# A hybrid encoder layer on one core: a pool for the ropes, z staging, u stores on ScalarE's queue and a pinned start

## The chip, the cores and the metric

The kernel runs on one core of a Trainium2 chip. A core has TensorE (PE, which multiplies matrices; its weight loads are listed apart as PEld), VectorE (DVE), ScalarE (ACT), GpSimd (POOL) and SyncE (SP), which work side by side and wait for one another by semaphores. DMA transfers are issued from the queues of SP, ACT and POOL. The metric is the device time of one execution in microseconds; given is the median of the runs. One further execution was profiled.

## The reference

One encoder layer is applied to two sequences, of 256 and 512 tokens (together 768 tokens, six tiles of 128), with the same parameters. The width is 1024, all in float32.

```python
h = rmsnorm(x); u, q, k, v, qm, gl = split(h @ w_in)
y = s5_forward(u) + s5_backward(u) + d * u          # 64 groups, 64 complex states each
z = gelu(y);  s5_out = z * sigmoid(z @ w_glu)
q, k = rope(rmsnorm(q)), rope(rmsnorm(k))           # 8 heads, each with two softmax maps
diff = rmsnorm((softmax(q1 k1) - lam * softmax(q2 k2)) @ v) * (1 - 0.2)
mem = softmax(rmsnorm(qm) @ rmsnorm(mem_k).T) @ mem_v     # 256 memory tokens for each sequence, 4 heads
merged = sum over the three branches of sigmoid(gl_n + b_n) * (branch_n @ w_branch_n)
x = x + merged @ w_out
x = x + (silu(g) * up) @ w_down,  where g, up = rmsnorm(x) @ w_gate_up
```

## The kernel before

Every dense product is made of three matmuls (`mm3`, L748): each factor is split into a high part (`hi`, rounded by ACT) and a low part (`lo`, the rest, by DVE), and hi*hi, hi*lo and lo*hi are summed in PSUM. Weights come through `WStream` (L504): `_dma` loads half a chunk (512 KB) on SP's queue, `_split` makes its two parts on ACT (L595) and DVE (L601), and `ahead` keeps loads and splits in front of their use.

The Python code is written in program order; the framework plans it. It follows a simulated time line and may let an instruction of an engine pass others that were written before it, where the data allow. The order so found is fixed in the program. `tc.keep_in_program_order` takes an instruction out of this freedom; `tc.issue_after` ties one behind another. A tile pool is a piece of on-chip memory with a fixed place: pools are stacked from the left and, with `side="right"`, from the right. A pool that is opened where a closed pool lay can be written only when the instructions that used the old one are done.

The stages, in order of time:

1. Start (L678 to L1016). Warm-up matmuls on the identity keep PE running (L678). The gain of the memory norm is transposed to a column (L982, L983). `mem_features` (L991) transposes the memory rows (`nT`), scales them with this column and splits them into `memThi` (ACT) and `memTlo` (DVE). `mem_k(0)` multiplies them with the first weights (`mk`).
2. Memory attention, with the projections of q and of u. `u_chunk` (L1070) computes u into a tile `ut` by groups (ACT or DVE copies out of PSUM), and `u_flush` (L280) stores the tile to a scratch in HBM. The first four tiles use a pool with two buffers, the last four a pool with one (`utp2`, L1097). PSUM kind "d", into which u goes, has three buffers.
3. The S5 scan, spread over the products of the gates (`gl`).
4. Differential attention. `qk_units` (L1180) projects q and k of a head, normalizes and rotates them into `rope` (L1195); `v_units` (L1212) projects v for two heads. `diff_attend` (L1257) is a generator that runs beside them, paced by `dat.tick`: `stack` transposes `rope` into `qst`, `kst` and `kl` (L1235), `scores` (`sc`, L1286), `transposes` (`aT`, L1309), `values` (`av`, L1323) and `finish` (`oT`, `do`, L1345 to L1347). `rope` lies in pool `dq1`; with `dq2` it belongs to `wctx`, which is closed after the last projection (L1422). The attention's other tiles belong to `dctx`.
5. The branches (L1494 on). `merged` (L1500, 24 KB in each of the 128 partitions) lies on the right, where `dq1` and `dq2` were. The memory branch (`branch(2, ...)`, L1584) runs together with the rest of the attention: its first chunk (L1526 to L1542) has four accumulators. Ahead of its last chunk `tail` (L1572) drains the attention, closes `dctx`, opens `x1` and `XB` and loads z from its scratch (`load_pair`, L1561, on POOL's queue) to split it. Rows 2, 3, 4 and 7 of z come through `zst`, three buffers of 3 KB for each partition, the others through `stg`. Then follow the gated product of z (`glu`), the other two branches, the output projection, and the feed-forward part.

Of the kernel before, what the change touches and what calls it, by code (L numbers as in the profile page):

```python
# [23 lines left out]
class S5:  # L24
# [255 lines left out]
    def u_flush(self, ut, mt):  # L280

        self.nc.sync.dma_start(self.u_scr[mt].rearrange("(j h) (g k) -> h g j k", j=8, k=NK), ut)
# [221 lines left out]
class WStream:  # L504
# [7 lines left out]
    def __init__(self, nc, tc, ctx):  # L512
        self.nc = nc
        self.praw = ctx.enter_context(tc.tile_pool(name="wraw", bufs=3))
        self.ph = ctx.enter_context(tc.tile_pool(name="whi", bufs=4))
        self.pl = ctx.enter_context(tc.tile_pool(name="wlo", bufs=4))
        self.sub = nc.vector
        self.by_dma = False
        self.half = None
        self.src = []  # L520
        self.raw = {}
        self.parts = {}
        self.n_dma = 0
        self.n_split = 0
        self.next = 0
# [57 lines left out]
    def _split(self):  # L583
        i, h = divmod(self.n_split, 2)
        self.n_split += 1
        kind = self.src[i][3]
        if kind == "w":
            return self._split_w(i, h)
        hi, lo = self.tiles(f"{i}_{h}")
        self.parts.setdefault(i, []).append((hi, lo))  # L590
        r = self.raw.pop(2 * i + h)
        if kind == "g":
            f = lambda t: t.rearrange("p (m h g) -> p m g h", h=16, g=8)
            hi, lo, r = f(hi), f(lo), r.rearrange("p (m g h) -> p m g h", g=8, h=16)
        self.nc.scalar.activation(hi, r, AF.Copy)  # L595
        if self.by_dma:

            self.nc.scalar.activation(lo, r, AF.Copy, scale=-1.0)  # L598
            self.nc.gpsimd.dma_start(lo, r.bitcast(F32R), accum_op=ALU.add)  # L599
            return  # L600
        self.sub.tensor_tensor(out=lo, in0=r, in1=hi.bitcast(F32), op=ALU.subtract)  # L601
# [25 lines left out]
def hybrid_block(ctx, tc, A, outs, consts):  # L627
# [51 lines left out]
    for _ in range(14):  # L679
        pe.matmul(warm[:, 0:128], env.ident, env.ident, start=True, stop=True)  # L680
# [295 lines left out]
    with tc.tile_pool(name="nrm", bufs=1) as pool, tc.tile_pool(name="nrmg", bufs=1) as pg:  # L976
# [5 lines left out]
        pe.transpose(ps[:, 0:8], grow, env.ident[0:8, 0:8])  # L982
        v.tensor_copy(gcol, ps[:, 0:8])  # L983
        xm = []
# [6 lines left out]
        def mem_features(t0, nt):  # L991
            nk = 4 // nt
            for k0 in range(0, 8, nk):
                ps = env.psb("nT")
                pv = ps.rearrange("p (k t) -> p k t", k=nk)
                for k in range(nk):
                    for t in range(nt):
                        c = 128 * (k0 + k)
                        pe.transpose(pv[:, k, 128 * t : 128 * t + 128], xm[t0 + t][:, c : c + 128], env.ident)
                for k in range(nk):  # L1000
                    sl = (slice(None), k0 + k, slice(128 * t0, 128 * t0 + 128 * nt))
                    split_evac(MT[0][sl], MT[1][sl], pv[:, k], gcol[:, k0 + k : k0 + k + 1])
                if t0 == 0:
                    W.ahead(0, 1 + k0 // 4)

        mem_features(0, 1)
        units = mem_k(0)
# [126 lines left out]
    k2 = dctx.enter_context(tc.tile_pool(name="da2", bufs=2))  # L1134
    q1 = wctx.enter_context(tc.tile_pool(name="dq1", bufs=1))
# [42 lines left out]
    RO, VV, ST, half = {}, {}, {}, {}  # L1178

    def qk_units(h):  # L1180
# [3 lines left out]
        for tt in range(TILES):  # L1184
# [7 lines left out]
            if tt == TILES - 1:  # L1192
                mean_eps(ss, TILES * 4, 64)
                rs = rsqrt(ss, TILES * 4, "qkrs")
                ro = q1.tile([128, TILES, 256], F32, name=uid("rope"), tag="rope")  # L1195
# [16 lines left out]
    def v_units(vp):  # L1212
        w = W.get()
        V = k2.tile([128, TILES, 256], F32, name=uid("V"), tag="V")
        VV[vp] = V
        for tt in range(TILES):
            ps = psd("v")
            dense_tm(ps, w, 0, 256, H, tt)
            act.activation(V[:, tt], ps[:, 0:256], AF.Copy)
            yield 1.0  # L1220
# [36 lines left out]
    def diff_attend():  # L1257
# [90 lines left out]

        for i in range(N + 5):
            h, tt = divmod(i, TILES)  # L1350
            while (i < N and h not in ST) or (2 <= i < N + 2 and (i - 2) // TILES // 2 not in VV):
# [142 lines left out]
    with ExitStack() as c5:  # L1494
# [64 lines left out]
        zst = zctx.enter_context(tc.tile_pool(name="zst", bufs=3, side="right"))  # L1559

        def load_pair(X, src, scale=None, more=()):  # L1561
# [10 lines left out]
        def tail(c):  # L1572
# [8 lines left out]
            load_pair(Z, z_scr, 0.5, (2, 3, 4, 7))  # L1581
# [367 lines left out]
```

## Time and profile before

| | us |
|---|---|
| median of 3 runs | 1748.81 (1747.99 to 1750.8) |
| the profiled execution | 1746.76 |
| its span, from the first to the last instruction | 1745.0 |
| busy in the span: PE, PEld | 1730.8, 1605.3 |
| busy in the span: DVE, ACT, POOL | 1262.2, 888.9, 269.7 |

In rows of a profile, L595 is a line of the kernel above; `wh<-wr` names the tile that is written and those that are read, without their numbers; x124 counts instructions. An engine's idle time is put down to what released it, as in `<-ACT wh L595`. A matmul's end is modelled, so one matmul looks longer than what it adds when others follow it closely. A DMA's row on a queue is its issue; its landing is told apart. The granted clock of TensorE was 1.000 over the execution.

### The profile page before, as it was taken

What the parts mean: (1) busy time and instruction counts of PE and PEld (TensorE: products, weight loads), DVE (VectorE), ACT (ScalarE), POOL (GpSimd) and SP (SyncE); (2) the same over time, 40 slices, a digit from 0 to 9 for tenths busy, and PEclk for the clock granted to TensorE, in tenths of its full rate; (3) what the DMA queues carried; (4) which work ended last, traced back from release to release, by engine and by line L of the source; (5) the groups of instructions that cost most, each with busy time, mean ns of one, the idle gap of its engine ahead of it and who ended that gap; (6) DMA issues with size and microseconds to landing.
All of it is one profiled execution on the core that took longest, in us unless ns stands there. A gap on an engine that the chain in (4) does not pass through costs nothing.

```text
span 1745.0 us, 29497 instructions
## 1 busy us (share of the span) xinstructions
PE 1730.8 (99%) x11236; PEld 1605.3 (92%) x11236; DVE 1262.2 (72%) x2353; ACT 888.9 (51%) x1868; POOL 269.7 (15%) x288
## 2 busy tenths in 40 slices
PE   9999999999999999999999999999999999999999
PEld 9999988999999999999989888888889999998887
DVE  7665649699999778887886445453598777776775
ACT  7444543776767346877765434232343333334443
POOL 0000000000000100111000002000036555541130
PEclk9999999999999999999999999999999999999999
DMA  7223636755566454645653437331312323238973
GB/s 270 75 85 97 127 114 132 182 125 147 143 159 159 115 143 101 161 97 153 165 164 109 133 115 249 116 117 62 87 65 91 109 91 109 91 110 283 259 159 95
DMA packets 209214, 234.11 MB, mean 134 GB/s; under 512 B 57832, under 2 KB 173296, under 8 KB 209072
## 3 DMA queue, kind: packets, MB, share of 16 engines
q1 hardware_dynamic: 190480, 170.73, 32.6%
q0 software_dynamic: 17440, 58.34, 15.4%
q10 hardware_dynamic: 1152, 3.15, 0.5%
q8 instruction: 89, 1.46, 0.4%
q14 instruction: 53, 0.43, 0.1%
HBM read 165.78 MB, written 41.22 MB: 119 GB/s over the span
## 4 chain that ended last, share of the span: by engine, by line
PE 95%; DVE 2%; DMA 1%; ACT 1%; issue 0%; SPq 0%; ACTq 0%
PE gl L751 4%; PE br L751 4%; PE br L752 4%; PE gl L753 4%; PE gl L752 4%; PE br L753 4%; PE gate L751 3%; PE up L751 3%; PE gate L753 3%; PE gate L752 3%; PE up L752 3%; PE up L753 3%; PE dn L752 3%; PE dn L753 3%; PE dn L751 3%; PE qk L752 3%
## 5 line engine op out<-in xcount | busy, mean ns | idle before, releaser
L595 ACT ACTIVATE wh<-wr 128x1024 fp32r<-128x1024 f32 x124 | 140.4, 1133 | 65.0 <-PE br L752 26.2
L601 DVE TENSOR_TENSOR wl<-wr,wh 128x1024 fp32r<-128x1024 f32 x82 | 108.5, 1324 | 81.8 <-ACT wh L595 80.0
L751 PE MATMUL gl<-H,wh 128*128 128x256 f32 (+1 forms) x384 | 132.0, 344 | 0.0
L753 PE MATMUL gl<-H,wl 128*128 128x256 f32 (+1 forms) x384 | 129.0, 336 | 0.0
L752 PE MATMUL gl<-H,wh 128*128 128x256 f32 (+1 forms) x384 | 128.7, 335 | 0.0
L599 POOL DMA_DIRECT2D wl<-wr x42 | 36.6, 872 | 504.7 <-ACT wl L598 486.9
L751 PE MATMUL qk<-wh,H 128*128 128x256 f32 x384 | 108.0, 281 | 0.0
L752 PE MATMUL qk<-wl,H 128*128 128x256 f32 x384 | 107.8, 281 | 0.0
L753 PE MATMUL qk<-wh,H 128*128 128x256 f32 x384 | 107.1, 279 | 0.0
L752 PE MATMUL dn<-wld,dxh 128*128 128x512 f32 x231 | 89.6, 389 | 0.0
L751 PE MATMUL dn<-whd,dxh 128*128 128x512 f32 x231 | 89.5, 389 | 0.0
L753 PE MATMUL dn<-whd,dxl 128*128 128x512 f32 x231 | 88.9, 389 | 0.0
L753 PEld LDWEIGHTS gl<-H,wl 128*128 128x128 f32 x384 | 72.0, 188 | 8.0
L752 PEld LDWEIGHTS gl<-H,wh 128*128 128x128 f32 x384 | 72.2, 188 | 7.2
L751 PEld LDWEIGHTS gl<-H,wh 128*128 128x128 f32 x384 | 72.3, 188 | 6.9
L557 ACT ACTIVATE wh_S<-ws 128x512 fp32r<-128x512 f32 x70 | 41.1, 625 | 65.2 <-PE up L752 36.8
L753 PEld LDWEIGHTS qk<-wh,H 128*128 128x128 f32 x384 | 72.3, 188 | 0.7
L751 PEld LDWEIGHTS qk<-wh,H 128*128 128x128 f32 x384 | 72.4, 188 | 0.6
L752 PEld LDWEIGHTS qk<-wl,H 128*128 128x128 f32 x384 | 72.2, 188 | 0.5
L1292 DVE TENSOR_REDUCE nm<-sc 128x1 f32<-128x512 f32 (+1 forms) x96 | 56.7, 597 | 18.4 <-PE sc L1287 17.6
L558 DVE TENSOR_TENSOR wl_S<-ws,wh_S 128x512 fp32r<-128x512 f32 x70 | 57.9, 850 | 15.9 <-ACT wh_S L557 15.9
L1294 ACT ACTIVATE p<-sc,nm 128x512 f32<-128x512 f32 (+1 forms) x96 | 58.8, 615 | 13.5 <-DVE nm L1292 13.0
(477 smaller groups left out, 6001.3 us busy)
## 6 DMA issues: line engine op xcount, KB each, us to landing
wr<-in_w_in_dram SPq DMA_DIRECT2D x48, 512.0 KB, 4.6
wr<-in_w_gate_up_dram SPq DMA_DIRECT2D x44, 512.0 KB, 3.6
wl<-wr POOLq DMA_DIRECT2D x42, 512.0 KB, 5.4
wr<-in_w_branch_dram SPq DMA_DIRECT2D x24, 512.0 KB, 4.7
glr<-gl_scr POOLq DMA_DIRECT2D x24, 384.0 KB, 3.9
hid_scr<-fa SPq DMA_DIRECT2D x11, 768.0 KB, 6.5
wr<-in_w_mem_kv_dram SPq DMA_DIRECT2D x16, 512.0 KB, 4.2
wr<-in_w_in_dram SPq DMA_DIRECT2D x32, 256.0 KB, 3.7
```

The lines of the kernel that those rows point to most:

```text
L557: self.nc.scalar.activation(f(hi), src, AF.Copy)
L558: self.nc.vector.tensor_tensor(out=f(lo), in0=src, in1=f(hi).bitcast(F32), op=ALU.subtract)
L595: self.nc.scalar.activation(hi, r, AF.Copy)
L599: self.nc.gpsimd.dma_start(lo, r.bitcast(F32R), accum_op=ALU.add)
L601: self.sub.tensor_tensor(out=lo, in0=r, in1=hi.bitcast(F32), op=ALU.subtract)
L751: pe.matmul(ps, wh, xh, start=start, stop=False, **kw)
L752: pe.matmul(ps, wh, xl, start=False, stop=False, **kw)
L753: pe.matmul(ps, wl, xh, start=False, stop=stop, **kw)
L1292: v.tensor_reduce(out=nm[:, m : m + 1], in_=ps, axis=AX.X, op=ALU.max, negate=True)
L1294: act.activation(pm[:, 0:n], ps, AF.Exp, bias=nm[:, m : m + 1], accum_out=s1s[:, tt : tt + 1] if m == 0 else s2)
```

## The change

Four things are changed, with what they need.

- `u_flush` issues its store from ScalarE instead of SyncE.
- The ropes get a pool of their own, `drope`, opened after `da2` and ahead of `dq1`, and closed with `dctx`.
- `zst` is no longer opened ahead of the memory branch but in `tail`, after `x1` and `XB`. Beside it, `diff_attend` asks for the tiles of V that a step reads (`values_there`), where it asked whether V was begun.
- At the beginning, nine of the 14 warm-up matmuls stay in their place and five follow the transpose of the gain; all of them and this transpose keep their order. For the first tile of the memory rows, the split of half a weight chunk is written ahead of the scaling of the four rows, and ACT's part of both keeps its order.

```diff
@@ u_flush
-        self.nc.sync.dma_start(self.u_scr[mt].rearrange("(j h) (g k) -> h g j k", j=8, k=NK), ut)
+        self.nc.scalar.dma_start(self.u_scr[mt].rearrange("(j h) (g k) -> h g j k", j=8, k=NK), ut)
@@ WStream
+        self.mark = lambda i: None
...
-        self.nc.scalar.activation(hi, r, AF.Copy)
+        self.mark(self.nc.scalar.activation(hi, r, AF.Copy))
@@ hybrid_block
     warm = env.psa("warm")
-    for _ in range(14):
-        pe.matmul(warm[:, 0:128], env.ident, env.ident, start=True, stop=True)
+
+    def warming(n):
+        for _ in range(n):
+            tc.keep_in_program_order(pe.matmul(warm[:, 0:128], env.ident, env.ident, start=True, stop=True))
+
+    warming(9)
...
-        pe.transpose(ps[:, 0:8], grow, env.ident[0:8, 0:8])
+        tc.keep_in_program_order(pe.transpose(ps[:, 0:8], grow, env.ident[0:8, 0:8]))
         v.tensor_copy(gcol, ps[:, 0:8])
+        warming(5)
@@ mem_features
+                if t0 == 0:
+                    W.ahead(0, 1 + k0 // 4)
                 for k in range(nk):
                     sl = (slice(None), k0 + k, slice(128 * t0, 128 * t0 + 128 * nt))
-                    split_evac(MT[0][sl], MT[1][sl], pv[:, k], gcol[:, k0 + k : k0 + k + 1])
-                if t0 == 0:
-                    W.ahead(0, 1 + k0 // 4)
-
+                    gk_ = gcol[:, k0 + k : k0 + k + 1]
+                    hi = act.activation(MT[0][sl], pv[:, k], AF.Copy, scale=gk_)
+                    if t0 == 0:
+                        tc.keep_in_program_order(hi)
+                    v.scalar_tensor_tensor(out=MT[1][sl], in0=pv[:, k], scalar=gk_, in1=MT[0][sl].bitcast(F32),
+                                           op0=mul, op1=sub)
+
+        W.mark = tc.keep_in_program_order
         mem_features(0, 1)
+        W.mark = lambda i: None
@@ pools of the attention
     k2 = dctx.enter_context(tc.tile_pool(name="da2", bufs=2))
+    rop = dctx.enter_context(tc.tile_pool(name="drope", bufs=1))
     q1 = wctx.enter_context(tc.tile_pool(name="dq1", bufs=1))
@@ qk_units
-                ro = q1.tile([128, TILES, 256], F32, name=uid("rope"), tag="rope")
+                ro = rop.tile([128, TILES, 256], F32, name=uid("rope"), tag="rope")
@@ v_units
         VV[vp] = V
+        V_TILES[vp] = 0
         for tt in range(TILES):
...
             act.activation(V[:, tt], ps[:, 0:256], AF.Copy)
+            V_TILES[vp] = tt + 1
             yield 1.0
@@ diff_attend
+        def values_there(i):
+            if not 0 <= i < N:
+                return True
+            h, tt = divmod(i, TILES)
+            return V_TILES.get(h // 2, 0) >= (2 if tt < 2 else TILES)
+
         for i in range(N + 5):
             h, tt = divmod(i, TILES)
-            while (i < N and h not in ST) or (2 <= i < N + 2 and (i - 2) // TILES // 2 not in VV):
+            while (i < N and h not in ST) or not values_there(i - 2):
                 yield
@@ the branches
         zctx = c5.enter_context(ExitStack())
-        zst = zctx.enter_context(tc.tile_pool(name="zst", bufs=3, side="right"))
-
-        def load_pair(X, src, scale=None, more=()):
+        def load_pair(X, src, scale=None, zst=None, more=()):
...
             Z = L["Z"] = pair(L["XB"], "z")
-            load_pair(Z, z_scr, 0.5, (2, 3, 4, 7))
+            zst = zctx.enter_context(tc.tile_pool(name="zst", bufs=3, side="right"))
+            load_pair(Z, z_scr, 0.5, zst, (2, 3, 4, 7))
             zctx.close()
```

More of the change, by code (lines that the diff above doesn't have):

```diff
@@ L1177, in hybrid_block @@
         gp.memset(t[64 - 64 * (i % 2) : 128 - 64 * (i % 2)].bitcast(F32), 0.0)
-    RO, VV, ST, half = {}, {}, {}, {}
+    RO, VV, ST, half, V_TILES = {}, {}, {}, {}, {}
     def qk_units(h):
```

## The prediction

> **What bounds the kernel now.** I read the page first, then busy time in stretches of 25 us, then the waits of PE (TensorE).
>
> ```profile
> span 1745.0 us, 29497 instructions
> PE 1730.8 (99%) x11236; PEld 1605.3 (92%) x11236; DVE 1262.2 (72%) x2353; ACT 888.9 (51%) x1868; POOL 269.7 (15%) x288
> ```
>
> PE is busy for 1730.8 of 1745.0 us. No edit changes what PE computes, so the change can win little more than the 14.2 us in which PE stands still, plus what PE loses while busy but badly overlapped. In the next rows the first number after the comma of a window is its length, then comes the busy time of PE, PEld (weight loads), DVE, ACT and POOL.
>
> ```profile
> 0.00:25.00 25.00, 21.67 (x159) 20.96 (x160) 13.96 (x33) 15.87 (x37) 0.71 (x6) 1.00 0.83 286
> 275.00:300.00 25.00, 22.94 (x137) 20.09 (x137) 24.60 (x54) 8.67 (x13) 1.61 (x11) 1.00 0.50 114
> 875.00:900.00 25.00, 24.01 (x191) 22.93 (x189) 22.70 (x53) 16.85 (x47) 1.11 (x2) 1.00 0.60 186
> 900.00:925.00 25.00, 22.95 (x160) 20.03 (x161) 21.75 (x57) 19.20 (x56) 3.86 (x7) 1.00 0.45 130
> 1725.00:1750.00 25.00, 15.86 (x70) 12.78 (x69) 5.95 (x8) 1.89 (x3) 0.00 (x0) 0.93 0.09 32
> ```
>
> The idle time stands in four places: 3.3 us at the start, 2.1 us in 275 to 300, 0.99 + 2.05 = 3.0 us in 875 to 925, and 25 - 15.86 - 5 (the span ends at 1745) = 4.1 us at the end, which no edit touches. These four are 12.5 of the 14.2 us.
>
> ```profile
> PE u L751 <- ACT ut L1080: 2.1, 1, 2.1
> PE nT L999 <- DMA nx<-in_mem_prompt_dram: 1.5, 1, 1.5
> PE warm L680 <- POOL ident masks.py:199: 1.4, 1, 1.4
> PE mk L753 <- DVE memTlo L746: 0.4, 1, 0.4
> ```
>
> **Ropes in a pool of their own.** In before, the rotated q and k of a head (`rope`, L1195) lie in `dq1`, and `merged` (L1500) is laid over `dq1` and `dq2` once these are closed. So the first merge (L1520) may not write before PE has transposed the last head's `rope` (L1235).
>
> ```profile
> L1235 PE MATMUL qkT<-ident,rope x96: 270/272/303, 650.3 to 910.0; 128*128 128x128 f32 x96
> L1520 DVE SCALAR_TENSOR_TENSOR merged<-glr,br x16: 376/552/689, 911.3 to 987.4; 128x256 f32<-128x256 f32 x8, 128x512 f32<-128x512 f32 x8
> L1208 DVE TENSOR_TENSOR rope<-rope,ropet x16: 648/950/1246, 638.6 to 889.6; 128x512 f32<-128x512 f32 x8, 128x1024 f32<-128x1024 f32 x8
> 880.00:896.00 16.00, 16.00 (x130) 15.57 (x130) 15.55 (x32) 8.73 (x24) 1.11 (x2) 1.00 0.72 222
> 896.00:912.00 16.00, 12.96 (x84) 10.06 (x83) 11.90 (x37) 14.27 (x46) 1.42 (x3) 1.00 0.08 28
> 912.00:928.00 16.00, 16.00 (x116) 14.94 (x115) 14.14 (x34) 9.43 (x22) 2.44 (x5) 1.00 0.72 214
> L1323 PE MATMUL av<-V,aT 128*128 128x128 f32 x32 | 4.7, 286 | 1.6 <-ACT aT L1311 1.6
> L1286 PE MATMUL sc<-kst,qst 128*128 128x512 f32 (+1 forms) x10 | 4.2, 424 | 0.6 <-ACT p L1294 0.6
> L752 PE MATMUL br<-H,wh 128*128 128x256 f32 x1 | 0.4, 365 | 0.0
> ```
>
> ```profile
> 890.17 0.12 PE br L752
> ```
>
> The rows fit: last transpose at 910.0, first merge at 911.3. The first chunk of the branch wants four PSUM accumulators (L1531 to L1535) and the kind "d" has three, so from 896 the branch stands still (one `br` matmul on L752 in 896 to 912) and PE runs attention alone, waiting for ScalarE. With the change, what `merged` covers is `dq1` without `rope` and `dq2`; their last use is L1208 at 889.6 + 1.2 = 890.8. The merges can then go from about 891, and three of the chunk's six products of 256 columns are still to be done: 3 x 24 matmuls at 0.12 us (what one adds to the chain of waits when others stand before and behind it, the row above; 365 ns is only its modelled length) is 8.6 us of filler, more than the gaps.
>
> What is won lies between 16.00 - 12.96 = 3.0 us (PE's plain idle time in 896 to 912) and 16.00 - 10.06 - 0.43 = 5.5 us (idle time of the weight loads, less the 0.43 us that they miss in 880 to 896). It can also be zero, if the branch only runs ahead and attention then ends as late as now. I take **4.0 us**, nearer the plain idle time. Lost against it are two merges of 0.4 us that DVE must now fit in earlier; DVE has 11.90 of 16 us there. The Trainium skill (Perfetto Trace Analysis, § Identifying the Most-Contended Engine) says that busy matmul time flatters PE and that weight-load time is the better measure; by it alone this term would be 5.5 us and the time 1.5 us lower. The two measures do part here (12.96 against 10.06 us busy); no run so far shows which of them a filled gap follows.
>
> **u stored by ScalarE's queue.** `u_flush` (L282) moves eight stores from SP's queue to ACT's. In the right-hand pool `utp2` there is one `ut`, so ACT may write the next only when the store has landed.
>
> ```profile
> 279.35 0.59 ACT L1080 ACTIVATE ut<-u 128x512 f32<-128x512 f32 x1
> 280.91 0.37 SPq L539 DMA_DIRECT2D wr<-in_w_in_dram  x1
> 281.39 8.10 DMA u_scr<-ut
> 289.58 0.88 ACT L1080 ACTIVATE ut<-u 128x256 f32<-128x256 f32 x2 [9.65 <-DMA u_scr<-ut]
> DMA to landing us min/median/max: 4.3/4.9/8.1
> L1347 ACTq DMA_DIRECT2D br_scr<-do x8: 326/326/344, 740.7 to 985.8; - x8
> ```
>
> `ut` is full at 279.94, but SP holds the store behind a weight load that itself waits for a buffer; it leaves at 281.39, lands 8.1 us later, and PE has waited 2.1 us. On ACT it can leave at 280.0, ahead of that load. Landing after 4.3 to 8.1 us gives 284.3 to 288.1; PE goes on when the first of the two copies at 289.58 ends, near 290.0, and has been ready since 290.0 - 2.1 = 287.9. With 0.4 us for a copy, the late landing leaves 0.6 us of the wait, the early one none: 1.5 to 2.1 us go. What ACT pays is 8 x 0.33 = 2.6 us of issue over some 80 us, in a stretch where it is busy for 8.67 of 25 us; queued behind an issue are weight splits and `ut` copies, each late by 0.33 us, for which PE waits next; with ACT idle for 16 of 25 us I let them be caught up. The bounds are 0 and 2.1 us. I take **2.0 us**. The rule against it: the Trainium skill (DMA: Bandwidth & Descriptors, § Issuing engines are not separate DMA queues) has transfers from all queues interleave on the same 16 engines, so that another queue saves issue time alone. By it the store still needs 8.1 us, this term is 1.5 us and the time 0.5 us higher; no row here separates the two.
>
> **Pinned order at the beginning.** Nine of 14 warm-up matmuls, then the transpose of the gain, then five; the first weight splits of ACT are planned before the four `memThi` of their half instead of anywhere, and their order is kept.
>
> ```profile
> 1.38 5.67 PE L680 MATMUL warm<-ident 128*128 128x128 f32 x28 [1.38 <-POOL ident masks.py:199]
> 7.03 1.06 ACT L595 ACTIVATE wh<-wr 128x1024 fp32r<-128x1024 f32 x1 [5.00 <-DMA wr<-in_w_mem_kv_dram]
> 8.45 1.06 ACT L595 ACTIVATE wh<-wr 128x1024 fp32r<-128x1024 f32 x1 [0.35 <-DMA wr<-in_w_mem_kv_dram]
> 9.52 0.63 ACT L745 ACTIVATE memThi<-nT,gmem 128x128 fp32r<-128x128 f32 x2
> ```
>
> ```profile
> 9.27 0.16 DVE L983 COPY gmem<-gT 128x8 f32<-128x8 f32 x1
> ```
>
> ```profile
> 8.20:11.10 2.90, 0.95 (x8) 0.72 (x7) 2.79 (x5) 2.10 (x5) 0.00 (x0) 1.00 1.00 400
> ```
>
> Nine of 14 take 5.67 x 9 / 14 = 3.6 us, so the gain's column is there at about 1.38 + 3.6 + 0.2 + 0.2 = 5.4 instead of 9.4, if its load has landed by 5.0; a later landing costs at most what the last five warm-ups are pushed past 7.1. ACT ends its first split at 8.1 and now does four `memThi` (0.31 us each) at once, where it waited for the second load until 8.45 and split it first: the first one at 8.1 instead of 9.52. But DVE is busy for 2.79 of 2.90 us in 8.2 to 11.1, and what it must do (two low parts, then the `memTlo`) is the same. So PE may fill its idle 1.5 + 0.4 us, or meet DVE's limit two microseconds later and win nothing. It could lose 1.2 us, four `memThi` ahead of the second split. I take **1.0 us** between.
>
> **z staging behind the attention.** `zst` is opened in `tail` after `x1` and `XB`, since three buffers of 768 x 4 bytes are 9 KB and the 6 KB of ropes now lie there.
>
> ```profile
> 910.55 1.71 POOL L1565 DMA_DIRECT2D brr<-z_scr  x3 [19.93 <-PE qkT L1235]
> 984.72 1.04 ACT L1346 ACTIVATE do<-oT,subg 128x256 f32<-128x256 f32 x2
> 986.38 3.04 ACT L745 ACTIVATE zhi<-brr 128x768 fp32r<-128x768 f32 x4
> ```
>
> ```profile
> L746 DVE SCALAR_TENSOR_TENSOR zlo<-brr,zhi x8: 948/950/959, 986.5 to 995.2; 128x768 fp32r<-128x768 f32 x8
> ```
>
> ```profile
> DMA to landing us min/median/max: 3.4/4.5/10.3
> ```
>
> ```profile
> 987.20:1004.00 16.80, 16.80 (x97) 14.70 (x97) 1.25 (x3) 1.00 0.70 222
> ```
>
> Three z loads go at 910.55 today, released by the same last rope transpose. At best the new place waits for the same thing; at worst for attention's end, the last `do` at 984.72 + 1.04 = 985.8. A load then lands at 985.8 + 4.5 = 990.3, ACT and DVE split it in 0.84 + 0.95, by 992.1; the gated product takes 16.8 / 8 = 2.1 us for a row of z, so from 987.2 it wants row 2 at 991.4. Cost 0.7 us at the median landing, 6.5 us at the longest (10.3). I take zero: the release is the same. The stricter test on V (`values_there`) asks for tiles that must have been written already for the result to be right; it delays nothing and I cost it at zero, at worst one unit of V (8 x 3 x 0.12 = 2.9 us) of other PE work earlier.
>
> **Sum.** 4.0 + 2.0 + 1.0 = 7.0 us. The profiled execution took 1746.76 us (1745.0 of span, 1.8 around it), 2.05 us under the median of 1748.81. So 1739.8 for such an execution and **1741.8 us** for the median.
>
> **Rivals.** (a) *The ropes win nothing*: the merges still wait for something else in that place, or ACT, busy for 14.27 of 16 us in 896 to 912, keeps attention's pace, and the branch that ran ahead is missing later. Then 3.0 us are left: 1745.8. For it: that ACT row. Against it: ACT has 9.43 of 16 us afterwards, so attention can catch up. (b) *Slower*: attention's end becomes the bound. The branch, used up at 896 to 912, no longer covers 976 to 987, and the four z loads issued only at 985.8 stand in that chain at their longest landing. 4.0 us of gain go, 6.5 us are added: 1746.76 - 3.0 + 6.5 + 2.05 = 1752.3, and 1754 if the eighth row, which waits for the third's buffer, costs 2 us more. It decides once the third z row lands after 991.4 - 1.8 = 989.6 and the branch has run dry before 985. Against it: today's loads wait for the rope alone. (c) *More*: 5.5 + 2.1 + 1.9 = 9.5 us: 1739.3, or less by what a newly planned order takes from attention elsewhere.
>
> **Chances.** Forecast 0.55 (own range 1739.8 to 1744.5), (a) 0.20, (b) 0.13, (c) 0.12. A measurement tells about 0.2%, 3.5 us, from no change: faster is below 1745.3, slower above 1752.3. Faster 0.55 + 0.12 + 0.03 of (a) = 0.70; same 0.17 of (a) and 0.03 of (b) = 0.20; slower 0.10. The range, 1738.0 (c less the 0.8 us by which the runs fall under their median, rounded) to 1748.5, holds the forecast, (a) and most of (c).
>
> **What would show it.** The first merge near 891 and `br` matmuls throughout 896 to 912, PE busy for nearly 16 of 16 us; no wait of `u` for `ut`; stores of u issued within 0.2 us of the copy; first `memThi` near 8.1; z loads near 905. A PE wait on `zlo` or `br` dry before 985 would make it wrong, as would new PE waits in places that no edit names.

## The result, and the profile after

The changed kernel takes 1753.22 us (median of 8 runs, 1751.87 to 1755.92), the kernel before 1748.45 us on the same chip (8 runs, 1747.99 to 1750.8). The ratio is 1.0029, 95% interval 1.0018 to 1.0040: some 5 us slower, where 7 us faster were forecast. Here and below a ratio compares a kernel with the kernel before in the same batch, is not quite the quotient of the two medians, and leaves out one slow execution of u alone (2438 us, granted clock 0.66).

The page of the changed kernel:

```profile
span 1753.7 us, 29486 instructions
PE 1736.8 (99%) x11236; PEld 1612.3 (92%) x11236; DVE 1265.0 (72%) x2353; ACT 890.0 (51%) x1868; POOL 269.0 (15%) x288
```

PE works on the same 11,236 matmuls, but counts as busy for 6.0 us more (1736.8 against 1730.8) and stands still for 16.9 us instead of 14.2. (The two profiled executions lie 8.75 us apart, 1755.51 against 1746.76, the medians only 4.8, so part of what this trace loses belongs to this one execution.) Where that is shows in its stretches of 25 us (columns as in the prediction; the number in front of the last two is the granted clock):

```profile
0.00:25.00 25.00, 20.35 (x115) 18.83 (x115) 10.87 (x26) 12.66 (x30) 0.71 (x6) 0.86 0.83 284
275.00:300.00 25.00, 25.00 (x147) 22.00 (x146) 23.34 (x77) 8.98 (x16) 0.55 (x9) 1.00 0.51 94
875.00:900.00 25.00, 25.00 (x202) 24.30 (x202) 21.25 (x51) 14.92 (x43) 1.11 (x2) 1.00 0.75 230
900.00:925.00 25.00, 25.00 (x188) 23.61 (x187) 17.47 (x47) 17.00 (x46) 1.65 (x3) 1.00 0.29 92
975.00:1000.00 25.00, 18.31 (x95) 15.81 (x94) 13.53 (x30) 11.96 (x25) 1.61 (x3) 0.80 0.35 121
```

The last of these stretches before the change:

```profile
975.00:1000.00 25.00, 25.00 (x143) 21.80 (x142) 15.72 (x29) 10.22 (x13) 2.69 (x5) 1.00 0.46 146
```

The two gaps that the change aimed at in the middle are closed: 22.94 became 25.00 in 275 to 300, and 875 to 925 is full. But the start has fewer matmuls (115 against 159) at a lower clock, and a new hole stands in 975 to 1000, which was full before. Three of the longest waits of PE name both places:

```profile
PE oT L1361 <- DVE osb L1353: 5.2, 1, 5.2
PE glu L756 <- ACT zhi L750: 1.5, 1, 1.5
PE mk L758 <- DVE memTlo L1014: 1.4, 1, 1.4
```

**The new hole, in order of time** (start, duration, engine, line, operation, idle time before it and what ended it):

```profile
983.97 0.39 PE L758 MATMUL br<-H,wl 128*128 128x512 f32 x1
...
984.21 1.05 PE L1339 MATMUL av<-V,aT 128*128 128x128 f32 x8
...
986.41 0.16 DVE L1348 TENSOR_TENSOR ssq<-ssq,r 128x6 f32<-128x6 f32 x1
...
989.42 0.96 DVE L1353 TENSOR_TENSOR osb<-osb,rqy 128x768 f32<-128x768 f32 x1
...
990.43 1.54 PE L1361 MATMUL oT<-ident,osb 128*128 128x128 f32 x6 [5.18 <-DVE osb L1353]
...
992.01 0.69 ACT L1362 ACTIVATE do<-oT,subg 128x512 f32<-128x512 f32 x1 [0.38 <-PE oT L1361]
992.60 0.83 ACT L750 ACTIVATE zhi<-brr 128x768 fp32r<-128x768 f32 x1
...
993.49 1.65 PE L756 MATMUL glu<-zhi,wh 128*128 128x256 f32 x4 [1.51 <-ACT zhi L750]
...
997.06 0.63 PE L758 MATMUL glu<-zhi,wl 128*128 128x512 f32 x1
```

The last `br` matmul goes at 983.97, the attention's last `av` right behind it. Then only the end of the attention is left, one thing after another: sum of squares, small steps of DVE from 986.41 to 989.42, the scaling of `osb`, its transposes, `do`, and only then the split of z, which lies where the attention's tiles were. PE has nothing to put into it. In before the last `br` (L753) went at 987.0, behind the last `oT`, so this chain was covered:

```profile
L1345 PE MATMUL oT<-ident,osb x10: 272/272/273, 960.4 to 984.1; 128*128 128x128 f32 x10
```

```profile
L753 PE MATMUL br<-H,wl x144: 276/280/480, 879.6 to 987.0; 128*128 128x256 f32 x96, 128*128 128x512 f32 x48
```

And the matmuls behind the hole of the changed kernel are slow: 0.63 us for one of 512 columns at 997.06, 0.39 us at 983.97.

### The profile page after: what moved, and what is told of

It reads as the page before. It is cut to its first block, busy times and chain, and to the rows that moved or that the text cites. A ratio compares the mean times of both kernels' runs of the same rounds, so it can differ in the third digit from the quotient of the medians.

```text
span 1753.7 us, 29486 instructions
## 1 busy us (share of the span) xinstructions
PE 1736.8 (99%) x11236; PEld 1612.3 (92%) x11236; DVE 1265.0 (72%) x2353; ACT 890.0 (51%) x1868; POOL 269.0 (15%) x288
## 4 chain that ended last, share of the span: by engine, by line
PE 96%; DVE 1%; DMA 1%; ACT 1%; issue 0%; SPq 0%; DVEq 0%; ACTq 0%
PE gl L756 4%; PE gl L757 4%; PE gl L758 4%; PE br L756 4%; PE br L757 4%; PE br L758 4%; PE gate L756 3%; PE gate L758 3%; PE up L756 3%; PE up L758 3%; PE gate L757 3%; PE up L757 3%; PE dn L758 3%; PE dn L757 3%; PE dn L756 3%; PE qk L758 3%
## 5 line engine op out<-in xcount | busy, mean ns | idle before, releaser
L1308 DVE TENSOR_REDUCE nm<-sc 128x1 f32<-128x512 f32 (+1 forms) x96 | 56.5, 597 | 17.8 <-PE sc L1303 16.9
```

The source lines that it names most:

```text
L1308: v.tensor_reduce(out=nm[:, m : m + 1], in_=ps, axis=AX.X, op=ALU.max, negate=True)
```

## The experiments

All kernels contain the edit to u's store, so what the other parts do is read against the first of them, u alone.

**1. The parts by themselves.** u's store alone:

```
-        self.nc.sync.dma_start(self.u_scr[mt]..., ut)
+        self.nc.scalar.dma_start(self.u_scr[mt]..., ut)
```

> The kernel before with the u store on ScalarE's queue alone. Theory: 2.1 us gained, 1748.45 - 2.1 = 1746.3, ratio 0.9988; the store that takes 8.1 us is issued within 0.3 us of its copy and PE does not wait for ut. Rival, that transfers interleave anyway and only the issue is earlier: 1.5 us, and PE still waits 0.6 us.

Measured: 1746.10 us, ratio 0.9989 (0.9979 to 0.9999). Run again in a later batch:

> u's store alone once more, beside the last one on the same chip: 0.9985 to 0.9993 of before.

Measured: 1745.34 us, ratio 0.9997 (0.9988 to 1.0006), above what was expected. Between them it wins 0.5 to 1.9 us; with two kernels below whose other edit shows no cost (0.9993 and 0.9992) the mean is 0.0007, 1.3 us. Its window, without a wait of PE for `ut`:

```profile
275.00:300.00 25.00, 25.00 (x145) 22.00 (x145) 24.60 (x54) 8.79 (x13) 2.48 (x11) 1.00 0.49 102
```

The store that took 8.1 us before, and the copy that waits for its landing:

```profile
280.13 0.37 ACTq L282 DMA_DIRECT2D u_scr<-ut  x1
286.84 0.88 ACT L1080 ACTIVATE ut<-u 128x256 f32<-128x256 f32 x2 [6.80 <-DMA u_scr<-ut]
```

It leaves within 0.1 us of its copy (279.45 + 0.60 = 280.05) and lands at most 6.7 us later. Five profiles with this store on ScalarE's queue (u alone twice, ropes and u, u with the pinned start, the changed kernel) have 5.7 to 6.7 us from its issue to the next copy. So it leaves sooner and also lands faster than the 8.1 us before; why it lands faster is not shown.

u's store with the ropes and z's staging, the start as before:

```
+    rop = dctx.enter_context(tc.tile_pool(name="drope", bufs=1))
-                ro = q1.tile(...)
+                ro = rop.tile(...)
-            while ... (i - 2) // TILES // 2 not in VV:
+            while ... not values_there(i - 2):
-        zst = zctx.enter_context(...)            # ahead of the branch
+            zst = zctx.enter_context(...)        # in tail, behind XB
```

> The change without its pinned start (u on ScalarE, ropes, z staging stay). Theory from the two traces: the pinned start costs 5.8 us (PE ends the first products at 157.6 instead of 151.8), so the time is 1753.2 - 5.8 = 1747.4, ratio 0.9994, and the first 25 us are as in the kernel before, granted clock 1.00. Rival, that the start is only shaken by a new plan and the pins as such cost nothing: 1753 again.

Measured: 1750.34 us, ratio 1.0017 (1.0008 to 1.0027). The ropes are not a gain: against u alone they cost 1.0017 - 0.9989 = 0.0028, 4.9 us (4.2 us by the medians of that batch). The rows of two tiles tell the same without the start: from the first `br` matmul on `H` to the last `glu` matmul (first and last start on the right). u alone, tile by tile:

```profile
L751 PE MATMUL br<-H,wh x144: 275/280/477, 878.2 to 985.4; 128*128 128x256 f32 x96, 128*128 128x512 f32 x48
```

```profile
L753 PE MATMUL glu<-zhi,wl x128: 274/337/397, 986.8 to 1052.7; 128*128 128x256 f32 x64, 128*128 128x512 f32 x64
```

and with ropes and z's staging:

```profile
L751 PE MATMUL br<-H,wh x144: 275/280/482, 879.6 to 979.8; 128*128 128x256 f32 x96, 128*128 128x512 f32 x48
```

```profile
L753 PE MATMUL glu<-zhi,wl x128: 274/389/628, 991.4 to 1058.8; 128*128 128x256 f32 x64, 128*128 128x512 f32 x64
```

1052.7 - 878.2 = 174.5 us against 1058.8 - 879.6 = 179.2 us: 4.7 us more, as the runs have it. This stretch is the yardstick below (the expectations count to the end of the last matmul, 0.4 us more). The branch is done at 980, 5.6 us sooner, and the product of z begins later. The yardstick is itself good to about 1 us: the second profile of u alone has 175.5 us, with the granted clock down to 0.93 in 900 to 925 where the first has 1.00.

u's store with the pinned start, no ropes (the other half of the change):

> The change without ropes and z staging (u on ScalarE and the pinned start stay). Theory: ropes with z staging cost 4.9 us net, because attention's end is left without cover; without them 1753.2 - 4.9 = 1748.3 and PE waits in 896 to 912 as before, none near 985. Rival, that the wait near 985 comes from everything being later: it stays, 1753.

Measured: 1748.76 us, ratio 1.0005 (0.9996 to 1.0014). The pinned start costs 0.0016, 2.8 us; added last (1.0029 less 1.0017) 2.1 us. Each part measured against u alone, the sum is -1.9 + 4.9 + 2.8 = 5.8 us, and 0.0029 of 1748 is 5.1: within the noise of these ratios the parts add up.

u's store with z's staging alone:

```
-        zst = zctx.enter_context(...)            # ahead of the branch
+            zst = zctx.enter_context(...)        # in tail, behind XB
```

> u's store, and the staging of z opened only behind the attention, as in the change; the ropes stay where they were before and the start is as before. Theory (the late opening costs nothing, the splits of z wait for the attention's memory in any case): 1745.6 to 1746.8, ratio 0.9985 to 0.9994, as u's store alone. Rival (the three loads of z now come late and the product of z waits for them): 1748 to 1752, ratio 1.000 to 1.0023, with a PE wait at the product of z.

Measured: 1745.93 us, ratio 0.9993 (0.9984 to 1.0002), its stretch from `br` to `glu` 174.5 us as with u alone. The late opening costs nothing that can be seen.

**2. Is it the pace of the attention?** Ropes and u, and the generator of the attention ticked faster beside the branch:

```
-DIFF_TAIL = 1.2
+DIFF_TAIL = 1.5
```

> As no_pins, with the attention paced 1.5 instead of 1.2 steps for each unit of the memory branch. Theory: what the ropes win at 896 to 912 (6 us) is lost because the branch is used up before attention ends; a faster pace keeps branch work for the end, so the PE wait for osb near 985 shrinks by half or more and the time is 1741 to 1744. Rival, z staging or the new pools make the end late by themselves: the wait stays near 5 us and the time near 1747.

Measured: 1750.09 us, ratio 1.0014 (1.0005 to 1.0023), a miss. PE's waits from 975 to 1000 are those of the change to the tenth: 5.2 us for `osb`, 1.5 us for `zhi`. The constant sets where attention stands in the Python text; what stands beside it on PE the framework's planning decides, and it spread the branch over the attention as before: 100.3 us from the first to the last `br` (on L751), 100.2 us with ropes and u. The edit did not touch the suspected cause, so the miss says nothing against it.

**3. What the wait costs beside itself.** Ropes and u; behind the attention's last `av`, matmuls of the identity into a free accumulator, which change no output:

```
+            if i == N + 2:
+                wt = env.psa("sc")
+                with tc.issue_after(AV[0].ins):
+                    for _ in range(44):
+                        pe.matmul(wt[:, 0:128], env.ident, env.ident, start=True, stop=True)
```

> Ropes and u's store, start as before, and 44 matmuls of the identity behind the attention's last product, which fill most of the wait for osb and change no output. The wait stays, only TensorE does not stand still in it. Theory (of the 12.6 us lost at the attention's end about half is the wait of 6.7 us and the rest the clock that falls after it): the granted clock of 975 to 1000 goes from 0.80 to 0.95 or more, and the time falls by 4 to 6 us from 1750.3 to 1744.5 to 1746.5, ratio 0.998 to 0.999. Rival (the slow matmuls there come from what they wait for, such as their operands, and not from the idle time): the time stays at 1749.5 to 1751.5, ratio 1.001 to 1.002.

Measured: 1753.37 us, ratio 1.0031 (1.0020 to 1.0043), a miss: the granted clock of 975 to 1000 was 1.00, but each of the 44 became two instructions, which ran until 989.6, while `osb` was ready near 985. With 20 in place of 44:

> As the run with 44 matmuls of the identity, with 20: the trace of that run shows 44 taking 10 us, twice what was meant, so that the transposes of osb came 4.7 us after osb was ready. 20 take 4.6 us and end ahead of osb; no output is changed. Theory (the clock that falls after the wait costs by itself; the product of z took 67.4 us from first to last matmul with the filler and 69.4 without): the granted clock of 975 to 1000 is 0.95 or more, the time 1.5 to 2.5 us below 1750.3, so 1747.8 to 1748.8, ratio 0.9998 to 1.0005. Rival (the slow clock comes anyway or costs nothing): 1749.8 to 1751, ratio 1.001 to 1.0017.

Measured: 1748.79 us, ratio 1.0008 (0.9998 to 1.0017), 0.0009 or 1.6 us below the run without the filler: the median as the theory had it, the ratio between the theory's range and the rival's, and the two intervals overlap. The trace is clearer: the stretch is 176.5 us instead of 179.2. Its window:

```profile
975.00:1000.00 25.00, 22.76 (x147) 20.00 (x146) 15.02 (x28) 12.36 (x20) 2.69 (x5) 1.00 0.41 137
```

The chain of `osb` and z is as long as without the filler, so 1.6 to 2.7 us of the loss are put down to the slow matmuls behind an idle PE.

**4. Cover for the attention's end.** Ropes and u; the matmuls of the branch's last chunks queued behind late scores. The first of four ways:

```
+    SC = {}
+    HOLD = {(2,0,0): 42, (2,0,1): 44, (2,1,0): 47, (2,1,1): 47, (3,0,0): 47, ...}   # (chunk, m, segment): tile
...
+                SC[i] = pe.matmul(ps, q[m][:, tok], kl[m][:, c0 : c0 + n], start=False, stop=True)
...
+                        with ExitStack() if late is None else tc.issue_after(SC[late].ins):
                             dense_fm(ps, w, m, X, c0, n, between=between)
...
-            if c != 3:
+            if c == 2:
+                dat.drain()
+            if c != 3:
                 return
-            dat.drain()
```

> Ropes and u's store as in the change, the start as before; the attention is drained ahead of the third chunk of the memory branch instead of the fourth, and the matmuls of its last two chunks are queued behind late scores (tile 42, 44 and 47 of 47), so that a third of the branch is left when the attention ends. Theory (the ropes let the branch run ahead, it is used up at the attention's end, and TensorE then waits 5.2 us for osb and falls to half clock): no wait for osb over 1 us and granted clock 1.00 in 975 to 1000, the time 6 to 9 us below the run of ropes and u without the pinned start (1750.3), so 1741 to 1744, ratio to before 0.996 to 0.998. Rival (the attention's end is late because its own steps on VectorE and ScalarE are slower with the ropes in place): the wait stays, 1749 to 1752, ratio 1.001 to 1.002. Second rival (holding back only moves the stall to the middle of the attention): waits of 3 us or more in 900 to 960, 1746 to 1748.

Measured: 1745.42 us, ratio 0.9986 (0.9976 to 0.9996): 5.4 us under ropes and u without it, but short of the theory's 0.996 to 0.998. The wait for `osb` is gone, but too much was held at once:

```profile
PE sc L1293 <- ACT p L1301: 2.4, 2, 2.2
```

Spread out (tiles 41, 43, 45, 46 for the third chunk):

> Ropes and u's store, the start as before; the holding back spread out: the third chunk's products behind the scores of tiles 41, 43, 45 and 46, the fourth chunk's behind tile 47 of 47. Theory (the attention's end needs a quarter of the branch as cover and the wait of 2.4 us in the middle came from holding too much at once): no PE wait over 1 us from 875 to 1015, granted clock 1.00 there, 1741 to 1744, ratio 0.9965 to 0.9982: faster than before and than u's store alone (1746.1). Rival (attention and branch together are bound by more than TensorE's cover; what is held back is lost in small waits): waits of 2 us or more remain somewhere between 900 and 1000, 1744.5 to 1747, ratio 0.998 to 0.9995.

Measured: 1744.76 us, ratio 0.9990 (0.9981 to 0.9998), stretch 173.3 us: in the rival's range. Now the middle is nearly free (1.1 us in two waits of `av`), and the end waits:

```profile
PE glu L751 <- ACT zhi L745: 1.9, 1, 1.9
```

> As the spread-out holding back, with the last part of the third chunk also behind tile 47, so that about a third instead of a quarter of the branch is left when the scores end. Theory (the 4.0 us of the ropes are there to be had, and what was left of the attention's end was a wait of 1.9 us for zhi): no PE wait over 0.7 us at the product of z, 1742 to 1744, ratio 0.997 to 0.9985. Rival (each us won at the end is lost in the middle): ratio 0.9985 to 0.9995, with a wait of 1 us or more from 940 to 980.

Measured: 1745.99 us, ratio 0.9990 (0.9981 to 0.9999), stretch 173.1 us, the same wait of 1.9 us for `zhi`: again the rival's ratio, though without its wait in the middle (0.7 us in all).

> As the last, with the second chunk's last part held behind tile 39, the third chunk's third part behind tile 44, and the attention drained one chunk sooner. Theory: as the last, 1742 to 1744, ratio 0.997 to 0.9985. Rival: ratio 0.9985 to 0.9995.

Measured: 1747.34 us, ratio 0.9999 (0.9990 to 1.0008): the same wait, and more in the middle, a third miss. In all three the rest of the branch was placed ahead of the last `oT`: it delayed the transposes, and nothing was left behind them. So the last product was tied to both sides of `oT`:

```
+    HOLD = {..., (2,1,1): 47, (3,0,0): 47, (3,0,1): 47, (3,1,0): "av", (3,1,1): "av"}
...
+                        if late == "av" and sg:
+                            for k in range(8):
+                                with tc.issue_after(SC["av" if k < 4 else "oT"].ins):
+                                    mm3(...)
```

> As the second spread-out holding back, with the last product of the branch also tied down: its first half behind the attention's last av, its second half behind the last oT, so that something is left both for the wait for osb (about 5 us) and for the copies of do and zhi behind it (about 2 us). Theory (the ropes' gain exists and was given back at the attention's end, where the branch was used up ahead of oT): no wait for zhi or osb over 1 us, 171.5 to 172.5 us from the branch's first to the product of z's last matmul (174.8 with u's store alone, 179.6 with the ropes and nothing held back), and a ratio of 0.9970 to 0.9985, 1.5 to 3 us below u's store alone in the same batch. Rival (what is won there comes back as waits in the middle): 174 us or more in that stretch and no difference from u's store alone.

Measured: 1741.87 us, ratio 0.9974 (0.9964 to 0.9984), 3.5 us below u alone in the same batch (4.0 us by the ratios), and below both the kernel before and the changed one. Its only wait of PE from 875 to 1000, and the two rows of the stretch:

```profile
PE av L1330 <- ACT aT L1318: 0.9, 3, 0.5
```

```profile
L751 PE MATMUL br<-H,wh x144: 275/280/482, 878.0 to 981.7; 128*128 128x256 f32 x96, 128*128 128x512 f32 x48
```

```profile
L753 PE MATMUL glu<-zhi,wl x128: 274/336/398, 983.0 to 1048.9; 128*128 128x256 f32 x64, 128*128 128x512 f32 x64
```

1048.9 - 878.0 = 170.9 us: 3.6 us less than u alone, 8.3 less than the ropes without cover. The theory holds, the rivals fall: the ropes' gain is real, and the attention's end took more than it gave. Holding the branch back without the ropes was not run; but u alone has its 3.1 us of PE waits from 875 to 1000 in the attention's steps (`av`, `sc`, `aT`, `qkT`) and none at the attention's end, so at the end there was nothing for a hold to win.

**5. The start.** The evacuations in pinned order without the divided warm-up, and the divided warm-up without the pinned evacuations, both with u's store on ScalarE's queue:

```
-        self.nc.sync.dma_start(self.u_scr[mt]..., ut)
+        self.nc.scalar.dma_start(self.u_scr[mt]..., ut)
...
+                if t0 == 0:
+                    W.ahead(0, 1 + k0 // 4)
...
+                    hi = act.activation(MT[0][sl], pv[:, k], AF.Copy, scale=gk_)
+                    if t0 == 0:
+                        tc.keep_in_program_order(hi)
```

> The change's start alone, without its warm-up: hi and lo of the memory rows by ScalarE and VectorE in pinned order, the next weight's split pinned ahead of them; all else as before. Theory (this order lets one PSUM bank pass between the two engines and delays the second weight's split by 3 us): the first weight product ends 3 us or more later and the time is 2 to 4 us above before, ratio 1.0012 to 1.0023. Rival (it is the divided warm-up, 9 matmuls at first and 5 behind the gain's transpose): 1747.5 to 1748.5 here, ratio 0.9997 to 1.0003.

```
-    for _ in range(14):
-        pe.matmul(warm[:, 0:128], env.ident, env.ident, start=True, stop=True)
+    warming(9)
...
+        warming(5)
```

> u's store by ScalarE's queue, and of the start only the warm-up: 9 matmuls ahead of the gain's transpose and 5 behind it, pinned; all else as before. Theory (the pinned evacuations cost the start, not the warm-up): as u alone, 1745.5 to 1746.7, ratio 0.9986 to 0.9993. Rival (the warm-up costs the 2.7 us): 1748 to 1749.5, ratio 1.000 to 1.001.

Measured: 1748.84 us, ratio 1.0007 (0.9997 to 1.0016), and 1746.25 us, ratio 0.9992 (0.9983 to 1.0002). The warm-up shows no cost. The first expectation says "all else as before" and counts from the kernel before, but its kernel has u's store in it too. Read against u alone (0.9989) the evacuations cost 0.0018 or 3.1 us, against the warm-up's kernel in the same batch 0.0015 or 2.6 us: all that the pinned start costs (2.1 to 2.8 us), and within the 2 to 4 us of the theory, whose ratio missed for the wrong base. The two intervals just overlap. The wait for `memTlo` in the evacuations' kernel:

```profile
PE mk L754 <- DVE memTlo L1009: 0.7, 1, 0.7
```

In its timeline ACT begins the second split at 11.91, as late as in the change (11.48, below), though the gain's column comes at 8.69, near the 9.27 of before and not the 5.83 of the change. So the pinned order delays the split, not the early column.

u's store and the whole pinned start, both halves of the first weight split first:

```
-                    W.ahead(0, 1 + k0 // 4)
+                    W.ahead(0, 2)
```

> u's store and the pinned start without the ropes, with one edit: both halves of the first weight are split ahead of the first evacuation, instead of the second half between the two groups of evacuations. Theory A (the late second split is what the pinned start pays for): the wait of 1.5 us for memTlo and most of the loss go, 1746 to 1747, ratio 0.9988 to 0.9994, near u's store alone (0.9989). Theory B (ScalarE and VectorE alternating on one PSUM bank is what it pays for, whatever the place of the split): 1748 to 1749.5, ratio 1.000 to 1.0008, as with the pinned start (1.0005).

Measured: 1746.41 us, ratio 0.9997 (0.9989 to 1.0006), by the ratio between the two theories (the median lies in A's range). The last one, and the pin on ScalarE's evacuations off:

```
-                    if t0 == 0:
-                        tc.keep_in_program_order(hi)
```

> u's store and the change's start with both halves of the first weight split ahead of the evacuations, and the pin on ScalarE's evacuations of the memory rows taken off; no ropes. Theory (the rest of what the pinned start costs is the alternation of ScalarE and VectorE on one bank, which the pin forces): the wait for memTlo is 0.5 us or less, the time as u's store alone, ratio 0.9985 to 0.9993. Rival (the rest comes from the place of the warm-up or from the splits ahead of the rows): ratio 0.9995 to 1.0003, with the same waits as with the pin (0.9997).

Measured: 1746.42 us, ratio 0.9993 (0.9984 to 1.0002), as expected. PE's wait for `memTlo` from 8 to 26 us, with the whole pinned start, with both halves split first, and with the pin off as well:

```profile
PE mk L758 <- DVE memTlo L1014: 1.5, 1, 1.5
```

```profile
PE mk L758 <- DVE memTlo L1014: 1.0, 2, 0.6
```

```profile
PE mk L758 <- DVE memTlo L1012: 0.4, 1, 0.4
```

From 1.0005 to 0.9997 to 0.9993, with u alone at 0.9989: the place of the second split looks like half of the cost, the pin like a quarter. The intervals overlap, so the shares are only indicated. Nor are the waits the whole cost: the evacuations by themselves wait 2.5 us in all from 8 to 26 (1.6 + 0.7 + 0.2) and u alone 2.3 (1.9 + 0.4); the rest would be in matmuls that run slower or less well overlapped. Which edit costs is shown, not how the cost divides.

## Why the prediction was wrong

**Ropes, 4.0 us forecast, 4.2 to 4.9 us lost.** The first steps held. Two tiles of the changed kernel, the transposes of `rope` and the first merges:

```profile
L1251 PE MATMUL qkT<-ident,rope x96: 270/272/273, 654.2 to 925.9; 128*128 128x128 f32 x96
```

```profile
L1542 DVE SCALAR_TENSOR_TENSOR merged<-glr,br x16: 402/550/689, 896.4 to 984.4; 128x256 f32<-128x256 f32 x8, 128x512 f32<-128x512 f32 x8
```

The first transpose of `rope` comes 3.9 us later than before (654.2 against 650.3): in this execution the last matmul of the first products (`mk`) starts 5.7 us later (157.3 against 151.6), and u's store wins part of that back. The merges begin at 896.4, long ahead of the last transpose at 925.9; the forecast, 891 + 3.9 = 894.9, was 1.5 us early. And the gap was worth what was said: 3.6 us in the stretch of the last hold, with 0.9 us of waits left in it: between the plain idle time of 3.0 and the 5.5 us of the weight loads. The Trainium skill (Perfetto Trace Analysis, § Identifying the Most-Contended Engine) calls matmul busy time a bad measure and prefers weight-load time; taken as the price of this one gap, weight-load time came out 1.9 us too high, of which the 0.9 us of waits may be a part.

The step that failed is the one that let the gain stand: "It can also be zero, if the branch only runs ahead and attention then ends as late as now". Zero was taken for the floor. The argument against rival (a), that ACT has room after 912 "so attention can catch up", failed with it: in the planned order branch matmuls stand between the attention's, and there room on ACT did not help. The last transpose of `rope` goes at 925.9 against 910.0, 12.0 us later after the shift of 3.9, and the branch is used up before the last `av`. In before the waiting merges had, without meaning to, kept the branch back as cover for the attention's end. Without cover that end costs 5.2 + 1.5 us of wait and 1.6 to 2.7 us of slow matmuls, 8.3 to 9.4 in all; the 3.6 us gained leave a loss of 4.7 to 5.8, measured 4.7 in the traces and 4.2 to 4.9 in the runs. This is the first half of rival (b), whose condition, the branch "run dry before 985", came true at 984; it was given 0.13. That its time, 1752.3, lies near the measured 1753.22 is luck: its price was 6.5 us for late loads of z, which did not come, and it knew nothing of the uncovered chain's 8 to 9 us or of the start's loss.

**z's staging, nothing forecast, nothing found.** With the ropes in their old place it cost nothing (0.9993). In the changed kernel the first three loads of z were again released by the last rope transpose, at 926.4, not near 905 as the text would have it, since that transpose had moved; they were long there when ACT took five splits in a row from 992.60. The second half of rival (b), 6.5 us for late loads, did not come.

**u's store, 2.0 us forecast, 0.5 to 1.9 measured.** The mechanism was right: the wait of 2.1 us has vanished from the trace, and the loss on ACT is too small to see. By the Trainium skill's rule (DMA: Bandwidth & Descriptors, § Issuing engines are not separate DMA queues) only the earlier issue would have been saved, 1.5 us. The trace does not agree in this place: the store also landed in at most 6.7 us instead of 8.1, and no wait of 0.6 us was left. The runs, with a mean of 1.3 us, cannot tell 1.5 from 2.0.

**Pinned start, 1.0 us forecast, 2.1 to 2.8 lost.** The bound "it could lose 1.2 us, four `memThi` ahead of the second split" failed. The first `memThi` did come early, at 7.87 where 8.1 was forecast. But the changed kernel's timeline goes on like this:

```profile
7.84 1.22 DVE L602 TENSOR_TENSOR wl<-wr,wh 128x1024 fp32r<-128x1024 f32 x1 [1.85 <-ACT wh L596]
7.87 0.37 ACT L1011 ACTIVATE memThi<-nT,gmem 128x128 fp32r<-128x128 f32 x1
8.98 0.34 DVE L1014 SCALAR_TENSOR_TENSOR memTlo<-nT,gmem,memThi 128x128 fp32r<-128x128 f32 x1
9.36 0.37 ACT L1011 ACTIVATE memThi<-nT,gmem 128x128 fp32r<-128x128 f32 x1 [1.12 <-DVE memTlo L1014]
...
11.48 1.05 ACT L596 ACTIVATE wh<-wr 128x1024 fp32r<-128x1024 f32 x1
...
15.54 1.22 DVE L602 TENSOR_TENSOR wl<-wr,wh 128x1024 fp32r<-128x1024 f32 x1
...
17.33 0.84 PE L758 MATMUL mk<-wh,memTlo 128*128 128x256 f32 x2 [1.45 <-DVE memTlo L1014]
```

The four were priced at 0.31 us each, as if ACT could do them at once. The second had to wait 1.12 us for DVE's `memTlo` of the first, which was itself held up by the low part of the weight. By the program both read the same `nT` tile, and the pinned order gave ACT no other tile to go to; in before, and with the pin off, the first two `memThi` run back to back. The Trainium skill (PSUM — Partial Sum Buffer, § PSUM bank collisions raise a hardware error) says that accesses of two engines to one bank have to be kept apart; the rows agree for the first tile, where ACT and DVE take turns from 7.87 to 9.73. That this is the reason for the wait is argued from the program, not shown by a run. The second split came at 11.48 instead of 8.45, 3.0 us late instead of 1.2, and the low parts of the next weights on DVE then fell ahead of the `memTlo` that PE needed at 15.9. DVE's load, which the text named ("meet DVE's limit two microseconds later"), was the right place with the wrong price.

**The sum.** Of the terms 4.0 + 2.0 + 1.0, one held in sign; the other two were gains whose loss side had been set at 0 and 1.2 us. The range ended at 1748.5 and missed the time by 4.7 us. (Its lower end should have been 1739.3 - 0.8 = 1738.5, not 1738.0; that changes nothing here.)

## What to carry to other kernels

A stall can be the cover of something later: before closing one with filler work, count the filler and look for the chain that it hides at its end; what is spent early must be held back there, by tying the last part of it behind the instructions between which PE would stand still. A constant that paces the text does not pace the engines when a planner orders them. Pinning one engine's order on a PSUM tile that a second engine also reads put their times in series here: price such a pin as a chain, with the work that stands ahead on the other engine, not as a sum of durations. And when an experiment is read, compare its kernel with the kernel that differs by the one edit: the evacuations' ratio of 1.0007 looked like almost nothing only against the kernel before.

## What was not expected of the hardware

The clock that TensorE is granted fell inside the kernel, in two places. The changed kernel's windows, with busy times of PE, PEld, DVE, ACT, POOL and then the clock:

```profile
13.00:17.00 4.00, 2.27 (x10) 1.44 (x10) 3.12 (x7) 1.88 (x5) 0.00 (x0) 0.95 0.98 371
17.00:19.00 2.00, 1.67 (x7) 1.67 (x8) 1.67 (x7) 1.62 (x5) 0.00 (x0) 0.50 1.06 362
19.00:21.00 2.00, 2.00 (x12) 2.00 (x11) 0.72 (x2) 0.68 (x2) 0.00 (x0) 0.50 1.10 348
...
985.00:989.00 4.00, 0.26 (x3) 0.07 (x1) 3.40 (x15) 0.91 (x4) 0.00 (x0) 1.00 0.34 113
989.00:993.00 4.00, 1.54 (x6) 1.15 (x6) 1.29 (x3) 1.46 (x3) 0.00 (x0) 0.55 0.12 40
993.00:997.00 4.00, 3.51 (x11) 3.10 (x12) 3.54 (x5) 3.36 (x5) 1.61 (x3) 0.50 0.51 182
997.00:1001.00 4.00, 4.00 (x17) 3.36 (x16) 2.19 (x4) 2.00 (x3) 0.54 (x1) 0.67 0.62 214
```

Late in the wait of 5.2 us the clock goes to 0.50, and it is full again only near 999.6, some 6 us after the product of z has begun (993.49): a wait at a tuned place costs more than its length, here 1.6 to 2.7 us more. The Trainium skill (TensorE: Matmul & The Clock Gate, § What's actually happening) states half clock after an idle window of about 3.4 us and full clock after as long a busy one, in windows that run freely. The second place agrees with that. At the start it does not: the clock falls to 0.50 at 17, and the longest single wait there was 1.45 us, though PE was busy for only 2.27 of the 4 us before. The clock of the start is also not the same in each execution: u alone, profiled twice, shows 1.00 and 0.93 in 0 to 25, and the last matmul of its first products starts at 152.4 and at 153.6. So what the lower clock adds at the start (0.86 in the profile of the change) could not be told from the waits, and is left open.
